# Layer 0's up projection with seven products for eight, its residual stream in DRAM during the MLP

## The chip, the cores and the metric

The kernel runs on one core of a Trainium2 chip (trn2). Its engines work side by side, each through its own instruction queue in order: TensorE (PE, matmuls), VectorE (DVE, elementwise work on tensors), ScalarE (ACT, functions and copies), GpSimd (POOL) and SyncE (SP), which issues most transfers. ACT and GpSimd can issue transfers too. The metric is the device time of one execution in microseconds (us); shorter is better.

## The reference

One inference step through two layers of a hybrid backbone, for 128 context tokens and 512 latent tokens, 640 in all, of 1024 channels. Each layer modulates its input with shift and scale rows made from a conditioning vector, projects it, runs three groups of heads (a two-way scan, a gated short convolution, a differential attention), projects back and adds:

```python
def trunk_layer(x, mod, p, ...):
    sh1, sc1, g1, sh2, sc2, g2 = jnp.split(mod, 6, axis=-1)
    u = x * (1.0 + sc1) + sh1
    m, k, v, s_f, s_b = mixer(u, p, ...)
    x = layer_norm(ALPHA * x + g1 * m, p['ln1_g'], p['ln1_b'])
    h = x * (1.0 + sc2) + sh2
    f = jnp.square(jax.nn.relu(h @ p['w_up'])) @ p['w_down']
    x = layer_norm(ALPHA * x + g2 * f, p['ln2_g'], p['ln2_b'])
    return x, k, v, s_f, s_b
```

`mod` is `silu(c) @ w_mod[l] + b_mod[l]`, with one `c` for the context tokens and one for the latent tokens; `w_mod[l]` is 1024 by 6144. The hidden width of the MLP is 4096. Everything is float32.

## The kernel before

Each float32 operand of a large product is split into a high part rounded to fp32r (by ACT) and a low part, the rest (a subtraction on DVE), and each product is three matmuls: high by high, high by low, low by high. `XH` and `XL` hold the split activations, channels on the partitions, tokens along the free axis. Weights come as 512 KB tiles through three `raw` buffers on SP's queue and are split into five buffers `hi` and `lo`.

`build` runs over the layers (L615). Its tools order each engine's instructions ahead of time, by a priority that follows the program's order; `tc.high_priority(offset=-LATE)` moves work behind. `fillers` are pieces of work that are threaded between others: `spread(n)` adds `n` to what is due and emits so many steps.

The end of a layer, which the change touches:

- Output projection `wo` (L1225 to L1232), in two blocks of 512 columns over five token tiles. `residual` multiplies the product with the gate row `grow` and adds the residual stream `res` (five tiles in SBUF, pool `rp`); `stats` makes mean and variance, with a power on GpSimd; `to_XT` transposes the normed tile into `XH`, `XL`. The LayerNorm's own scale and shift are applied to `res` later (`affine`, two DVE passes a tile).
- The MLP (L1441 on) goes through groups of hidden columns: up products, ReLU, square, split into `ah` and `al` (`squared`), then down products that are accumulated in `acc`.
  - Layer 0 (`fast` false): four groups of 1024, each of two plain up blocks (`up_block`: 192 matmuls, tokens as 384 + 256) and two down blocks (`tok_block`, one PSUM bank for each token tile, from the pair `mm`). The high part of the squares is a CAST on DVE (L1254).
  - Layer 1 (`fast` true): eight groups of 512. Group 0 is a plain up block, with the tokens as 320 + 320. Groups 1 to 7 are two calls of `fast_pair` each: the 2 x 2 block product of 256 hidden columns by 640 tokens, by halves of both and of the channels, with seven products (of 12 matmuls of 320 columns) for eight. It takes four sums of weights (`T1` to `T4`, made in each pair on DVE) and four sums of tokens. `token_sums` makes three of the latter once, in tiles `Sh`, `Sl` (the first two in `xn` buffers, six in `op`); `token_sums_in_place` writes the fourth over a quarter of `XH`, `XL`. `dn_fast` does the ten down products of a group, the first four halves in four PSUM banks (`mm` and `tp`).
- Layer 0 carries a filler through its MLP: `mod_steps_sum` makes seven modulation pieces (one of layer 0, six of layer 1) on DVE. Each of 112 tiles `ws` (256 KB, three buffers) is multiplied with two conditioning values and added into two accumulators `ma` (tag `xn`, two buffers): 28 first steps with one operand (L104), 196 with two (L109). PE then sums a piece over the partitions with a column of ones (`pmod`) and transposes it (`mod_tail`).
- At the last group, `acc` is multiplied by the second gate row and added to `res` (L1462 to L1465); the last down products come on top, with the LayerNorm. Layer 0 writes the result to `xspill` in DRAM, prepares layer 1's input (`put_u`) and starts its first product (`kv1`).

Of the kernel before, what the change touches and what calls it, by code (L numbers as in the profile page):

```python
# [35 lines left out]
FZ, FU, FD = 2, .7, 3  # L36
# [5 lines left out]
LATE, EARLY = 100, 50  # L42
# [3 lines left out]
ORDER, N_HALF = (4, 3, 0, 1, 2), 4  # L46
# [12 lines left out]
def build(ctx: ExitStack, tc: tile.TileContext, I, O):  # L59
# [159 lines left out]
    def mod_steps_sum(pieces, pool):  # L219
# [4 lines left out]
        def small(name):  # L224
            return pool.tile([P, 4, P], F32, tag="u", name=name, bufs=3).rearrange("p a b -> p (a b)")
# [11 lines left out]
        for l, pc in pieces:  # L237
            acc = [pool.tile([P, 1024], F32, tag="xn", name=f"ma{l}_{pc}_{s}", bufs=2) for s in range(2)]
# [220 lines left out]
    xspill = dp.tile([TOK, D], F32, name="xspill")  # L459

# [154 lines left out]
    for l in range(DEPTH):  # L615
# [553 lines left out]
        def stats(i, t):  # L1169
            mv = rp.tile([P, 4], F32, tag="mv", name=f"mv{l}_{i}_{t}", bufs=NT)  # L1170
# [5 lines left out]
        def stats_act(t):  # L1176

            mv = rp.tile([P, 4], F32, tag="mv", name=f"mv{l}_a{t}", bufs=NT)
# [37 lines left out]
        ubufs[0] = 5 if l + 1 == DEPTH else 3  # L1216
# [10 lines left out]
        if l + 1 < DEPTH:  # L1227
            next_end = ctx.enter_context(ExitStack())
            ep = next_end.enter_context(tc.tile_pool(name=f"kv{l + 1}", bufs=1, side=side_of(None), reuse_waits="tile"))
        op, op_end = open_pool("op")  # L1230
# [7 lines left out]
        fast = l + 1 == DEPTH  # L1238
        ng = 8 if fast else 4
        hg = 4 * D // ng  # L1240
        extra = {} if fast else {"more": op, "early": EARLY}
# [5 lines left out]
        def squared(r, hv, lv, src=None):  # L1247
# [12 lines left out]
        def up_block(g, b, ah, al):  # L1260
            blk = load_block(f"up{l}_{g}_{b}", w_up, 0, [(g * hg + b * 512, 512)], **extra)

            def ev_up(ct, half, ps):
                nm = f"relu{l}_{g}_{b}_{ct}_{half}"
                if fast:
                    o, m, r = half * H, H, room(nm)
                else:
                    o, m = (0, NA) if half == 0 else (NA, NB)
                    r = op.tile([P, NA], F32, tag="relu", name=nm, bufs=3)[:, :m]
# [3 lines left out]
            ch_block(f"up{l}_{g}_{b}", blk, ev_up, na=H if fast else NA)  # L1273
# [54 lines left out]
        def s_tile(name):  # L1328
# [83 lines left out]
        def dn_fast(g, stat, blks, evs):  # L1412

            items = [(t, c) for c in range(2) for t in ORDER]
            if g == ng - 1:
                items.sort(key=lambda x: ORDER.index(x[0]))
# [22 lines left out]

        ends = []  # L1440
        for g in range(ng):  # L1441
            ah, al = a_tiles(g, hg // P)
            if fast and g:
                for j in range(2):
                    fast_pair(g, j, ah, al)
                if g == ng // 2:
                    gate_rows(1)
            else:
                for b in range(hg // 512):
                    up_block(g, b, ah, al)  # L1450
                    if g == 0 and b == 0:
                        with tc.high_priority(offset=-LATE if fast else 0):
                            for t, mv in later:
                                affine(rows, t, mv)
                        if fast:
                            with tc.high_priority(offset=-LATE):
                                token_sums()
                    if g == ng // 2 and b == 0:
                        gate_rows(1)
                if fast:  # L1460
                    token_sums_in_place()
            if g == ng - 1:  # L1462
                for t in range(NT):
                    tt(acc[t], acc[t], grow[min(t, 1)], ALU.mult)
                    stt(res[t], res[t], ALPHA, acc[t], ALU.mult, ALU.add)  # L1465
                rows = norm_rows(1)
                if l + 1 < DEPTH:
                    fill_all()
                    make_aff(l + 1, 0, vt[:, 75:83], vt[:, 83:91])
            for cbi in range(2):  # L1470
                blk = load_block(f"dn{l}_{g}_{cbi}", w_down, g * hg, [(cbi * 512, 512)], nu=hg // 256, **extra)
# [5 lines left out]
                def ev_dn(t, ps, cbi=cbi, cs=cs, g=g):  # L1477
# [6 lines left out]
                    else:  # L1484
                        quiet = fast and t in ORDER[:-1]
                        residual(t, cbi, ps, None, not quiet)
                        if cbi == 1:
# [10 lines left out]
                            if l + 1 == DEPTH:  # L1498
                                end = t == ORDER[-1]
                                with tc.high_priority(offset=0 if end else -LATE):  # L1500
                                    finish(rows, 2 if end else 1)

                if fast:
                    ends.append((blk, ev_dn))
                else:
                    tok_block(f"dn{l}_{g}_{cbi}", blk, a_stat, ev_dn)
            if fast:
                dn_fast(g, a_stat, [e[0] for e in ends], [e[1] for e in ends])
                del ends[:]
# [67 lines left out]
```

## Time and profile before

| | |
|---|---|
| median of 3 runs | 1599.03 us (1595.26 to 1599.63) |
| the profiled execution | 1600.18 us, span of its records 1598.4 us |
| busy: PE, DVE, ACT, POOL | 1558.9, 1165.1, 768.6, 38.5 us |
| granted PE clock, mean | 0.995 of full speed |
| DMA | 201.47 MB, mean 126 GB/s |

PE rows give matmuls, PEld rows the loads of their stationary operand, which overlap them. Matmuls are pipelined and their ends are modelled, so the distance of their starts says more than their durations. L and a number is a line of the kernel; where a helper records all operations (L97 ACT copies and functions, L100 two-operand DVE passes, L109 scalar-tensor-tensor passes, L112 matmuls) the tile names say what it is. Layer 0's MLP runs from about 392 to 841 us, layer 1's from about 1167 to the end.

### The profile page before, as it was taken

To read this page: it belongs to the slowest core of one execution; us is meant where nothing else is said; L and a number is where in the kernel's file an instruction comes from. 1 tells how busy PE (TensorE), PEld (TensorE's weight loads), DVE (VectorE), ACT (ScalarE), POOL (GpSimd) and SP (SyncE) were. 2 spreads that over 40 slices of the span, in tenths; PEclk is the share of its full clock that TensorE was granted. 3 is DMA by queue.
4 is the path that set the end of the run, shared out by engine and by line. 5 is a ranking of instruction groups with operands and counts; after the bars stand their busy time and mean duration, and the time that the engine had idled before them with its cause. 6 is when DMAs were issued, how large, how long until landed. Compare 5 with 4: busy or idle time off the path is not lost.

```text
span 1598.4 us, 23756 instructions
## 1 busy us (share of the span) xinstructions
PE 1558.9 (98%) x9088; PEld 1373.1 (86%) x9088; DVE 1165.1 (73%) x2122; ACT 768.6 (48%) x1610; POOL 38.5 (2%) x68
## 2 busy tenths in 40 slices
PE   6999999999999999999999999999999999999997
PEld 3799957978989979979978999898798899988995
DVE  2589868778858478499376788898797566556687
ACT  3368735427422413314245587654486355434543
POOL 0000100000000000000000000000000000000001
PEclk9999999999999999999999999999999999999998
DMA  9641177342555355364226410524222233122311
GB/s 325 181 167 54 36 252 260 126 154 75 164 194 187 105 170 159 126 198 140 71 73 183 169 41 14 185 100 150 81 85 88 67 105 98 61 67 92 106 66 66
DMA packets 124833, 201.47 MB, mean 126 GB/s; under 512 B 10924, under 2 KB 57776, under 8 KB 124720
## 3 DMA queue, kind: packets, MB, share of 16 engines
q1 hardware_dynamic: 116592, 179.46, 35.0%
q10 hardware_dynamic: 8128, 20.50, 3.6%
q8 instruction: 71, 1.16, 0.3%
q14 instruction: 42, 0.34, 0.1%
HBM read 186.71 MB, written 13.22 MB: 125 GB/s over the span
## 4 chain that ended last, share of the span: by engine, by line
PE 86%; DVE 6%; DMA 3%; ACT 3%; issue 1%; POOL 1%; SPq 0%; DVEq 0%; ACTq 0%; POOLq 0%
PE dn_t L112 26%; PE up_c L112 15%; PE wo_t L112 4%; PE kv_t L112 4%; PE xb_c L112 4%; PE sa_c L112 3%; PE xa_c L112 3%; PE z_t L112 2%; PE pt L112 2%; PE px L1380 2%; PE px L1381 2%; PE px L1382 2%; PE dq_t L112 2%; PE pmod L112 2%; PE sb_c L112 2%; DVE res L109 1%
## 5 line engine op out<-in xcount | busy, mean ns | idle before, releaser
L112 PE MATMUL dn_t<-hdn,ah 128*128 128x512 f32 x640 | 251.2, 393 | 0.0
L112 PE MATMUL dn_t<-hdn,al 128*128 128x512 f32 x640 | 250.1, 391 | 0.0
L112 PE MATMUL dn_t<-ldn,ah 128*128 128x512 f32 x640 | 249.9, 390 | 0.0
L112 PE MATMUL up_c<-XH,hup 128*128 128x384 f32 (+2 forms) x576 | 178.3, 310 | 0.0
L112 PE MATMUL up_c<-XH,lup 128*128 128x384 f32 (+2 forms) x576 | 178.1, 309 | 0.1
L112 PE MATMUL up_c<-XL,hup 128*128 128x384 f32 (+2 forms) x576 | 178.1, 309 | 0.0
L109 DVE SCALAR_TENSOR_TENSOR ma<-ws,cstat,ma 128x512 f32<-128x512 f32 x196 | 138.1, 745 | 15.8 <-DMA ws<-in_w_mod_dram 15.1
L112 PEld LDWEIGHTS dn_t<-hdn,ah 128*128 128x128 f32 x640 | 120.2, 188 | 29.9 <-issue 2.5
L112 PEld LDWEIGHTS dn_t<-ldn,ah 128*128 128x128 f32 x640 | 120.2, 188 | 25.9
L112 PEld LDWEIGHTS dn_t<-hdn,al 128*128 128x128 f32 x640 | 120.2, 188 | 24.7
L112 PEld LDWEIGHTS up_c<-XH,lup 128*128 128x128 f32 x576 | 108.9, 189 | 0.8 <-DVE lup L100 0.7
L112 PEld LDWEIGHTS up_c<-XH,hup 128*128 128x128 f32 x576 | 108.1, 188 | 1.0 <-ACT relu L97 0.8
L112 PEld LDWEIGHTS up_c<-XL,hup 128*128 128x128 f32 x576 | 108.1, 188 | 0.5 <-DVE XL L100 0.2
L97 ACT ACTIVATE hdn<-rdn 128x1024 fp32r<-128x1024 f32 x64 | 66.9, 1053 | 79.7 <-PE dn_t L112 52.4
L100 DVE TENSOR_TENSOR ldn<-rdn,hdn 128x1024 fp32r<-128x1024 f32 x64 | 77.4, 1222 | 37.8 <-ACT hdn L97 37.7
L100 DVE TENSOR_TENSOR acc<-acc,dn_t 128x512 f32<-128x512 f32 x80 | 54.6, 683 | 56.5 <-PE dn_t L112 56.5
L97 ACT ACTIVATE relu<-up_c 128x384 f32<-128x384 f32 (+2 forms) x72 | 31.3, 434 | 112.1 <-PE up_c L112 105.0
L112 PE MATMUL wo_t<-hwo,XH 128*128 128x512 f32 x160 | 63.1, 394 | 1.5 <-ACT XH L97 1.5
L112 PE MATMUL wo_t<-hwo,XL 128*128 128x512 f32 x160 | 63.7, 398 | 0.0
L112 PE MATMUL wo_t<-lwo,XH 128*128 128x512 f32 x160 | 63.7, 398 | 0.0
L97 ACT ACTIVATE pe<-sc,zs 128x640 f32<-128x640 f32 (+1 forms) x80 | 56.8, 712 | 10.9 <-DVE pe L109 6.9
L844 DVE TENSOR_REDUCE zs<-sc 128x1 f32<-128x640 f32 x64 | 52.3, 820 | 12.5 <-PE sc L112 12.1
(413 smaller groups left out, 3913.2 us busy)
## 6 DMA issues: line engine op xcount, KB each, us to landing
rup<-in_w_up_dram SPq DMA_DIRECT2D x64, 512.0 KB
rdn<-in_w_down_dram SPq DMA_DIRECT2D x64, 512.0 KB
ws<-in_w_mod_dram SPq DMA_DIRECT2D x112, 256.0 KB
wm<-in_w_mod_dram SPq DMA_DIRECT2D x24, 512.0 KB
Ab<-adram SPq DMA_DIRECT2D x10, 1024.0 KB
rwo<-in_w_out_dram SPq DMA_DIRECT2D x16, 512.0 KB
wb<-in_w_mod_dram SPq DMA_DIRECT2D x12, 512.0 KB
kd<-hlks SPq DMA_DIRECT2D x40, 128.0 KB
```

Source lines behind the costliest of these rows:

```text
L97: S.activation(out=out, in_=in_, func=func, **kw)
L100: V.tensor_tensor(out=out, in0=a, in1=b, op=op)
L109: V.scalar_tensor_tensor(out=out, in0=a, scalar=s, in1=b, op0=op0, op1=op1, **kw)
L112: T.matmul(out, lhsT=l, rhs=r, start=start, stop=stop)
L844: V.tensor_reduce(out=nmax, in_=sv, axis=AX.XY, op=ALU.max, negate=True)
L1380: T.matmul(ps, lhsT=wh, rhs=xh, start=k == 0 and not more, stop=False, skip_group_check=more)
L1381: T.matmul(ps, lhsT=wh, rhs=xl, start=False, stop=False, skip_group_check=more)
L1382: T.matmul(ps, lhsT=wl, rhs=xh, start=False, stop=k == 3, skip_group_check=more)
```

## The change

Layer 0's MLP takes the form that layer 1 has: eight groups of 512, a plain up block in group 0, `fast_pair` in groups 1 to 7, `dn_fast` (now `dn_block`) for the down products. In both layers:

- after `affine` the five `res` tiles are written to DRAM (`mid`, on GpSimd's queue) and the pool `rp` is closed; a pool `sp` with six tiles `S0` to `S5` for the token sums takes its place;
- `before_last`, called between the two pairs of the last group, empties the fillers, loads the second gate rows, multiplies `acc` with them and adds ALPHA times the residual stream, which comes back from DRAM through the buffers `u` in halves of 512 columns (GpSimd's queue); `acc` then is `res`;
- the second LayerNorm's rows go into `S0` and `S1` (they went into `acc`);
- the gate rows share the buffers `ma` with the modulation sums, in `op`, which is opened ahead of the output projection (pool `gr` is gone); `ws` has a tag of its own.

The fillers are threaded otherwise (`FU` at each of four outputs of a pair, `FD` at each down product), the ring `u` has five buffers in both layers, layer 0's last group takes its token tiles in the order 0 to 4, and `EARLY` and the extra weight unit in `op` are gone. The diff, cut:

```diff
-FZ, FU, FD = 2, .7, 3
+FZ, FU, FD = 2, .8, 1.4
-ORDER, N_HALF = (4, 3, 0, 1, 2), 4
+ORDERS, N_HALF = ((0, 1, 2, 3, 4), (4, 3, 0, 1, 2)), 4
...
-            return pool.tile([P, 4, P], F32, tag="u", name=name, bufs=3).rearrange("p a b -> p (a b)")
+            return pool.tile([P, 512], F32, tag="ws", name=name, bufs=3)
...
-            acc = [pool.tile([P, 1024], F32, tag="xn", name=f"ma{l}_{pc}_{s}", bufs=2) for s in range(2)]
+            acc = [pool.tile([P, 1024], F32, tag="ma", name=f"ma{l}_{pc}_{s}", bufs=2) for s in range(2)]
...
+    mid = [dp.tile([TOK, D], F32, name=f"mid{l}") for l in range(DEPTH)]
...
-        gp, gp_end = open_pool("gr", "right")
+        op, op_end = open_pool("op")
...
-                r = gp.tile([P, D], F32, tag=f"grow{s}", name=f"grow{l}_{i}_{s}")
-                nc.scalar.dma_start(out=r, in_=gdram[l][i, s:s + 1, :].to_broadcast([P, D]))
+                r = op.tile([P, D], F32, tag="ma", name=f"grow{l}_{i}_{s}", bufs=2)
+                (nc.scalar, G)[i].dma_start(out=r, in_=gdram[l][i, s:s + 1, :].to_broadcast([P, D]))
...
-                r = acc[j]
+                r = acc[j] if i == 0 else sp.tile([P, D], F32, tag=f"S{j}", name=f"row{l}_{j}")
...
-        ubufs[0] = 5 if l + 1 == DEPTH else 3
+        ubufs[0] = 5
...
-        fast = l + 1 == DEPTH
-        ng = 8 if fast else 4
+        end = l + 1 == DEPTH
+        order = ORDERS[end]
+        ng = 8
...
-            if fast:
-                act(hv, r)
-            else:
-                V.tensor_copy(hv, r)
+            act(hv, r)
...
-                x = op.tile([P, 3 * H], F32R, name=name)
+                x = sp.tile([P, D], F32R, tag=f"S{len(made) - 3}", name=name)
...
             def out(r, ct, half, src=None):
+                spread(FU)
...
+        def before_last():
+            nonlocal rows
+            if l + 1 < DEPTH:
+                fill_all()
+            gate_rows(1)
+            for t in order:
+                a = acc[t]
+                tt(a, a, grow[min(t, 1)], ALU.mult)
+                for i in range(2):
+                    x, cs = flat(f"x{l}_{t}_{i}"), slice(i * 512, i * 512 + 512)
+                    G.dma_start(out=x, in_=mid[l][t * P:(t + 1) * P, cs])
+                    stt(a[:, cs], x, ALPHA, a[:, cs], ALU.mult, ALU.add)
+            res[:] = acc
+            rows = norm_rows(1)
+            if l + 1 < DEPTH:
+                make_aff(l + 1, 0, vt[:, 75:83], vt[:, 83:91])
...
-            if fast and g:
+            if g:
                 for j in range(2):
                     fast_pair(g, j, ah, al)
-                if g == ng // 2:
-                    gate_rows(1)
+                    if g == ng - 1 and j == 0:
+                        before_last()
...
-                        with tc.high_priority(offset=-LATE if fast else 0):
+                        with tc.high_priority(offset=-LATE):
                             for t, mv in later:
                                 affine(rows, t, mv)
+                                G.dma_start(out=mid[l][t * P:(t + 1) * P, :], in_=res[t])
+                        rp_end.close()
+                        sp, sp_end = open_pool("sp", "right")
+                        with tc.high_priority(offset=-LATE):
+                            token_sums()
...
-            if g == ng - 1:
-                for t in range(NT):
-                    tt(acc[t], acc[t], grow[min(t, 1)], ALU.mult)
-                    stt(res[t], res[t], ALPHA, acc[t], ALU.mult, ALU.add)
```

## Rows read from the trace of the kernel before

**Rows 1.** The page, part 1: busy time, share of the span and instructions of each engine.

```profile
PE 1558.9 (98%) x9088; PEld 1373.1 (86%) x9088; DVE 1165.1 (73%) x2122; ACT 768.6 (48%) x1610; POOL 38.5 (2%) x68
```

**Rows 2.** The chain of waits in order of time: start, length, what.

```profile
302.63 8.56 PE sb_c L112 x59
...
437.28 16.32 PE dn_t L112 x72
...
495.24 56.53 PE up_c L112 x384
...
841.31 10.99 PE kv_t L112 x48
...
1087.33 9.36 PE sb_c L112 x63
...
1194.82 27.48 PE dn_t L112 x120
1246.94 27.49 PE dn_t L112 x120
```

**Rows 3.** Busy time by stretch: length, PE, PEld, DVE, ACT, POOL, clock, DMA.

```profile
437.28:495.24 57.96, 57.96 (x267) 45.91 (x266) 36.28 (x56) 15.75 (x23) 0.00 (x0) 1.00 0.55 178
392.41:782.42 390.01, 389.57 (x2278) 351.77 (x2278) 279.07 (x456) 123.05 (x206) 0.00 (x0) 1.00 0.47 151
782.42:841.31 58.89, 57.80 (x266) 47.31 (x265) 40.76 (x62) 23.37 (x40) 1.62 (x3) 1.00 0.28 88
1167.54:1559.78 392.24, 392.24 (x2203) 357.14 (x2203) 263.04 (x430) 201.91 (x405) 2.05 (x1) 1.00 0.26 84
...
1507.54:1559.78 52.24, 52.24 (x289) 47.17 (x289) 41.56 (x58) 23.81 (x49) 0.00 (x0) 1.00 0.24 81
```

**Rows 4.** Grouped DVE instructions of layer 0's MLP, 395 to 841 us.

```profile
L109 DVE SCALAR_TENSOR_TENSOR ma<-ws,cstat,ma 128x512 f32<-128x512 f32 x196 | 138.1, 745 | 15.8 <-DMA ws<-in_w_mod_dram 15.1
...
L104 DVE TENSOR_SCALAR ma<-ws,cstat 128x512 f32<-128x512 f32 x28 | 11.9, 481 | 14.9 <-PE pmod L112 14.9
```

**Rows 5.** DVE in order of time in two dense runs: start, length, operation.

```profile
691.69 0.68 DVE L100 TENSOR_TENSOR acc<-acc,dn_t 128x512 f32<-128x512 f32 x1
692.29 1.41 DVE L109 SCALAR_TENSOR_TENSOR ma<-ws,cstat,ma 128x512 f32<-128x512 f32 x2
693.61 1.22 DVE L100 TENSOR_TENSOR ldn<-rdn,hdn 128x1024 fp32r<-128x1024 f32 x1
694.75 1.21 DVE L100 TENSOR_TENSOR lup<-rup,hup 128x1024 fp32r<-128x1024 f32 x1
...
1197.48 0.48 DVE L100 TENSOR_TENSOR Sl<-xa,Sh 128x320 fp32r<-128x320 f32 x1
1197.89 0.48 DVE L100 TENSOR_TENSOR xc<-xa,xc 128x320 f32<-128x320 f32 x1
```

**Rows 6.** Busy time by stretch, columns as in rows 3, of three dense runs.

```profile
1174.58:1217.44 42.86, 42.86 (x239) 38.45 (x238) 40.59 (x84) 30.51 (x63) 0.00 (x0) 1.00 0.18 58
686.06:725.43 39.37, 39.35 (x179) 31.48 (x179) 36.61 (x53) 7.62 (x8) 0.00 (x0) 1.00 0.63 197
...
664.14:724.94 60.80, 60.36 (x283) 47.94 (x283) 53.77 (x81) 12.55 (x16) 0.00 (x0) 1.00 0.61 191
```

**Rows 7.** Who waited for whom: us in total, times, longest.

```profile
DVE ma L109 <- DMA ws<-in_w_mod_dram: 15.1, 18, 2.0
DVE ma L104 <- PE pmod L112: 14.9, 4, 11.2
```

**Rows 8.** DVE in order of time, layer 1's first group.

```profile
1175.98 2.60 DVE L109 SCALAR_TENSOR_TENSOR res<-res,mv,acc 128x1024 f32<-128x1024 f32 x2 [0.51 <-ACT xn L97]
...
1189.21 0.48 DVE L100 TENSOR_TENSOR Sl<-xa,Sh 128x320 fp32r<-128x320 f32 x1
...
1215.97 1.47 DVE L100 TENSOR_TENSOR lo_T<-t,hi_T 128x512 fp32r<-128x512 f32 x2
```

**Rows 9.** The chain of waits, a weight tile of 512 KB.

```profile
350.45 4.29 DMA rup<-in_w_up_dram
```

More of the change, by code (lines that the diff above doesn't have):

```diff
@@ L1136, in build @@
         p1_end.close()
-        gp, gp_end = open_pool("gr", "right")
+        if l + 1 < DEPTH:
+            next_end = ctx.enter_context(ExitStack())
+            ep = next_end.enter_context(tc.tile_pool(name=f"kv{l + 1}", bufs=1, side=side_of(None), reuse_waits="tile"))
+        op, op_end = open_pool("op")
         grow = []
@@ L1169, in stats @@
         def stats(i, t):
[L1170 removed]
+            mv = op.tile([P, 4], F32, tag="mv", name=f"mv{l}_{i}_{t}", bufs=NT)
             V.bn_aggr(out=mv[:, 0:2], in_=st6[:, t].rearrange("p a b -> p (a b)"))
@@ L1176, in stats_act @@
         def stats_act(t):
-            mv = rp.tile([P, 4], F32, tag="mv", name=f"mv{l}_a{t}", bufs=NT)
+            mv = op.tile([P, 4], F32, tag="mv", name=f"mv{l}_a{t}", bufs=NT)
             x = op.tile([P, D], F32, tag="xn", name=f"dev{l}_{t}", bufs=2)
@@ L1260, in up_block @@
         def up_block(g, b, ah, al):
-            blk = load_block(f"up{l}_{g}_{b}", w_up, 0, [(g * hg + b * 512, 512)], **extra)
+            blk = load_block(f"up{l}_{g}_{b}", w_up, 0, [(g * hg + b * 512, 512)])
             def ev_up(ct, half, ps):
                 nm = f"relu{l}_{g}_{b}_{ct}_{half}"
[L1265 to L1269, printed above, removed]
+                o, m, r = half * H, H, room(nm)
                 squared(r, ah[4 * b + ct][:, o:o + m], al[4 * b + ct][:, o:o + m], ps)
                 spread(FU)
-            ch_block(f"up{l}_{g}_{b}", blk, ev_up, na=H if fast else NA)
+            ch_block(f"up{l}_{g}_{b}", blk, ev_up, na=H)
         quarter = {}
@@ L1410, in fast_pair, with dn_block @@
             out(room("c21" + nm), 0, 1, px)
-        def dn_fast(g, stat, blks, evs):
-            items = [(t, c) for c in range(2) for t in ORDER]
+        def dn_block(g, stat, blks, evs):
+            items = [(t, c) for c in range(2) for t in order]
             if g == ng - 1:
-                items.sort(key=lambda x: ORDER.index(x[0]))
+                items.sort(key=lambda x: order.index(x[0]))
             def part(i, ps, k0, k1):
@@ L1451, in build @@
                     if g == 0 and b == 0:
-                        with tc.high_priority(offset=-LATE if fast else 0):
+                        with tc.high_priority(offset=-LATE):
                             for t, mv in later:
                                 affine(rows, t, mv)
[L1455 to L1461, printed above, removed]
-            if g == ng - 1:
-                for t in range(NT):
-                    tt(acc[t], acc[t], grow[min(t, 1)], ALU.mult)
-                    stt(res[t], res[t], ALPHA, acc[t], ALU.mult, ALU.add)
[L1466 to L1469, printed above, removed]
+                                G.dma_start(out=mid[l][t * P:(t + 1) * P, :], in_=res[t])
[3 more added lines that the diff above has]
+                            token_sums()
+                token_sums_in_place()
             for cbi in range(2):
-                blk = load_block(f"dn{l}_{g}_{cbi}", w_down, g * hg, [(cbi * 512, 512)], nu=hg // 256, **extra)
+                blk = load_block(f"dn{l}_{g}_{cbi}", w_down, g * hg, [(cbi * 512, 512)], nu=hg // 256)
                 cs = slice(cbi * 512, (cbi + 1) * 512)
@@ L1484, in ev_dn @@
                     else:
-                        quiet = fast and t in ORDER[:-1]
+                        quiet = end and t in order[:-1]
                         residual(t, cbi, ps, None, not quiet)
@@ L1498, in ev_dn @@
                             if l + 1 == DEPTH:
[L1499 to L1509, printed above, removed]
+                                final = t == order[-1]
+                                with tc.high_priority(offset=0 if final else -LATE):
+                                    finish(rows, 2 if final else 1)
+                ends.append((blk, ev_dn))
+            dn_block(g, a_stat, [e[0] for e in ends], [e[1] for e in ends])
+            del ends[:]
         if l + 1 < DEPTH:
```

8 lines of the change are left out of this document (2 added, 6 removed).

## The prediction

> **What bounds the kernel now.** I read the page first: TensorE (PE) is busy 98% of the span, VectorE (DVE) 73% [rows 1]. An average over two layers says little about one stage, so I went on to the chain of waits. There the MLP of either layer is one unbroken run of matmuls: 384 up products in 56.53 us in layer 0, and in layer 1 down blocks of 120 products in 27.48 us that begin every 52.12 us [rows 2]. PE sets the end in both MLPs, and a product taken away is worth its time if nothing else becomes late. What could become late I read from the table of stretches: in layer 0's MLP DVE is busy 279.07 us of 390.01 up to the last down block, in layer 1's 263.04 of 392.24 [rows 3]. The grouped instructions say why layer 0 is so full although its MLP is the plain one: it also carries the weighted sums that make the modulation rows, 196 two-operand steps and 28 one-operand steps, 150.0 us together [rows 4]. Layer 1 has none. The question is whether layer 1's form of the MLP and these sums fit on DVE together.
>
> **The PE term.** One plain block of 512 hidden columns costs 56.53/2 = 28.27 us [rows 2]. The form with seven products costs what is left of layer 1's period: 52.12 - 27.48 = 24.64 us. Group 0 stays plain, so 7 groups x (28.27 - 24.64) = **25.4 us less**. The down products stay as many (8 groups of 120 for 4 of 240). The way into the MLP should not move: from the end of the last short-convolution product to the first down product layer 0 takes 437.28 - 311.19 = 126.1 us with two plain blocks inside, layer 1 takes 1194.82 - 1096.69 = 98.1 us with one [rows 2]; without that one block's 28.3 us the former is 97.8 us. So dropping `EARLY` and the extra unit in `op` is costed at nothing; what hides it is the PE work of the output projection, which is equally long in both.
>
> **The DVE term.** In a dense run what counts is the distance from start to start, since ends overlap: 0.40 us for 320 columns, 0.60 for 512, 1.14 for 1024, 0.66 for a modulation step of 512 [rows 5]; the one-operand step of a piece's first tile counts 0.40 (481 ns less the same overlap of 80) [rows 4], an `affine` pass 1.3 (2.60 for two) [rows 8]. I list what DVE must do in the changed layer 0 from the start of group 0's up block to the end of group 7's, by layer 1's counts:
> - 14 pairs, each 11 passes of 512 (four differences, seven low parts) and 7 of 320 (three sums, four low parts): 14 x 9.4 = 131.6
> - 56 passes of 320 for the token sums: 22.4
> - 32 splits of down weights x 1.14: 36.5
> - 60 accumulations x 0.60 (20 before): 36.0
> - group 0's low parts, the late `affine` passes and what is left of the projection: 13.0
> - gates and residual in `before_last`, 5 x 1.14 + 10 x 0.66: 12.3
> - modulation, 196 x 0.66 + 28 x 0.40 and small ones: 142.0
>
> Together 394 us. PE needs in the same stretch layer 1's 392.24 us [rows 3] and seven modulation pieces: layer 0's second stretch takes 57.96 us, with 2 x 27.48 = 54.96 of down products, some 0.7 of up and two pieces, so 1.15 us a piece [rows 2, 3], 8 us in all: 400.3 us. DVE would have to work **98% of the time** where it works 72% now. The casts of the squares go from DVE to ACT, and the list has none of them. ACT, with 23.81 of 52.24 us in a group of layer 1 [rows 3], has room, and costs nothing.
>
> How dense can DVE be? Two runs show it with all work ready: 40.59 of 42.86 us in layer 1's token sums and 36.61 of 39.37 in layer 0's modulation, so 94.7% and 93.0% [rows 6]. The gaps have two causes that stay: two accumulators `ma` for each piece, so that the next one waits for PE's column sum (14.9 us, 4 times), and three buffers `ws` (15.1 us, 18 times) [rows 7]. At these densities 394 us become 416 and 424, and PE would stand still for 16 to 23 us. The other end is nothing, since 394 is less than 400.3: a DVE that is late finds its inputs waiting, and a gap closes that in those runs only existed because nothing was due. I take **14 us**, nearer to the dense run that has the new form. Behind DVE the stall shows first at group 1, since the token sums and the first 20 modulation steps (6 in the up block, 14 in the down block) come ahead of its weights, where layer 1's run already ends only 5 us before the pairs begin at 1222.30 [rows 2, 8]; and at the end, where `gate_rows(1)` needs both `ma` and thus the last piece.
>
> **The last down block of layer 0.** It shrinks from 55 us to 27.5 and must take the same residuals. DVE is busy 40.76 us of the 58.89 at this place now [rows 3]; less half of the down splits (4 x 1.14) it has some 36 us of work for 27.5 of PE. PE runs on into `kv1` (10.99 us [rows 2]), which covers some of it. Bounds 0 and 8.5 us, the whole of the difference; taken: **4 us**.
>
> **The residual stream through DRAM.** Ten writes of 512 KB, twenty reads of 256 KB and four of the gate rows are issued by GpSimd, whose queue issues no transfer now and carries the power step of every LayerNorm. The writes gate the buffers `S`, which lie where `res` was. Landing bounds it: 512 KB of weights took 4.29 us [rows 9]. In layer 1 the last `affine` ends at 1178.6 and the first sums that would go into `S` come at 1189 [rows 8], so a write of 4.3 us is hidden with some 6 us to spare; late writes would hold the token sums, and these group 1. In `before_last` the x tiles come in among the five buffers `u` that the pair behind them also needs. Layer 1 does the same gates there now at no cost (52.24 us for the group, DVE 41.56 [rows 3]). Bounds 0 (all hidden) to 4.3 us a layer (one landing in the open); for both layers together **2 us**. `ma` for the gate rows of the first residual opens no new wait: its space is free once the scan is done, which comes before the projection.
>
> The Trainium skill speaks against this part. "SBUF — State Buffer", SBUF: two separate sides, says that a transfer issued by GpSimd has its descriptors written by that engine, and that a DVE copy, cast or one-operand step in SBUF locks it out meanwhile. The only ops of that kind left in layer 0's MLP would be the 28 one-operand steps of 481 ns, and no run of before has a GpSimd transfer that could show it; by the rule a write waits at most one such step, so the sum would be 1 to 2 us more.
>
> **Sum.** - 25.4 + 14 + 4 + 2 = - 5.4 us. The profiled execution took 1600.18 us, its span and 1.8 around it; it lies 1.15 us above the median of the three runs, 1599.03. Against itself 1594.8, against the median 1593.6: I forecast **1595 us**. About 0.3% (4.8 us) is what a measurement of this kernel can tell from no change, so the forecast stands at that edge.
>
> **Rivals.**
> 1. *DVE keeps up.* For it: in layer 1 no group loses PE time although its first stretch is 94.7% dense [rows 6], and there are five buffers for split weights, half a group of lead. Against it: 98% of the time is more than any run shows. Stall 0 to 5, little at the end: 1577 to 1586, say 1581.
> 2. *DVE becomes the bound and costs more than PE gives* (the other side). One mechanism: DVE's order is fixed, and a waiting step at its head (`ma` for PE, for `ws`) holds the weights of the next pair behind it. The longest stretch that is full, 664.14 to 724.94, has DVE at 53.77 of 60.80 us, 88.4% [rows 6]: 394 us would be 446, a stall of 45 and 1626 us. It decides from a density of 93.9% downward, where the stall passes 25.4 - 6 = 19.4 us, and from 92.8% by more than 0.3%. Against it: in that stretch DVE had no need to be denser, since PE waited for it almost nowhere. Typical 1612.
> 3. *The x reads come late.* They wait for buffers `u` and for GpSimd; each reads 256 KB behind the others. If ten of them land one after the other at half of 4.3 us each, they take 21 us from the moment at which the first buffer is free, of which the 24.64 us of the last pairs and the first half products hide all but what begins late. One landing of 4.3 us in the open at each layer's end, and as much for the token that follows: 8 us more than forecast, 1603.
> 4. *The seven column sums of the modulation stop PE,* because the down block now rotates through both pairs of PSUM banks and leaves none for them. One product group of 2.75 us (27.48/10) for each: 19 us, 1614. For it: `dn_block` takes four banks; against it: they are held for one matmul and one copy only.
>
> By a rule of "DMA: Bandwidth & Descriptors" in the Trainium skill, Anatomy of one DMA, a GpSimd transfer takes about 2 us and its bytes at 436 GB/s, an estimate of 2.6 us for 256 KB; ten in a row would be 26 us, and rival 3 is where that would show.
>
> **Chances.** Forecast 0.42 (stall 6 to 20 us: 1587 to 1601), rival 1 0.20, rival 2 0.23, rival 3 0.10, rival 4 0.05. The forecast's own range spans the edge: of its 0.42 half is faster by over 0.3%, 0.15 within, 0.06 slower. Rival 1 is all faster; rival 2 is slower but for 0.02; rival 3 is mostly within (0.06 to 0.04); rival 4 slower but for 0.01. That gives faster 0.41, same 0.24, slower 0.35. The range 1579 to 1614 leaves out the quicker third of rival 1 and the worse half of rival 2, a little under 2 in 10.
>
> **What will show it.** PE: pairs at 24.6 us where nothing is late, and 168 more lines of px, py and pz per group. DVE in layer 0's MLP over 90% in every group, where now 72%; if its busy share is high and PE's falls under 100% there, the DVE term is right, and the idle time of PE ahead of hi and lo tiles (or of `ma`) is its size. The last `ma` should stand in group 6 or 7, not, as now, one down block ahead of the end. Wrong would be: PE waiting on `S` tiles or on x (rivals 3), pairs that are slower by themselves, or DVE at a share under 90% with PE stalled. Layer 1 should be as long as before within 2 us.

## The result, and the profile after

| | before | after |
|---|---|---|
| median | 1599.3 us (4 runs, 1595.26 to 1599.63) | 1622.85 us (4 runs, 1620.29 to 1625.25) |
| span of the profiled execution | 1598.4 | 1618.3 |

The change makes the kernel slower: ratio 1.0148, 95% interval 1.0125 to 1.0172. The forecast was 1595 us, the range 1579 to 1614: wrong in sign, and outside the range. The profiled execution of the changed kernel, from which the numbers below come, is the shortest of its four: 1620.29 us at a mean granted clock of 0.992; the longest, 1625.25 us, shows 0.989.

The page of the kernel after, part 1, answers to [rows 1]: DVE is busy 78% of the span for 73, PE 96% for 98.

```profile
PE 1560.5 (96%) x8920; PEld 1353.8 (84%) x8920; DVE 1267.3 (78%) x2332; ACT 836.6 (52%) x1802; POOL 58.7 (4%) x102
```

Where the 19.9 us of the spans lie, by PE's starts. A is the stretch from layer 0's last short-convolution product (sb) to `kv1`, with the projection and the whole MLP; B from there to layer 1's last sb product; C layer 1's last group, from its first pair to the last down product. In brackets is what the granted clock took: the sum over windows of 10 us of length times (1 - clock).

| | A | B | C | the rest |
|---|---|---|---|---|
| before | 528.1 (0) | 257.4 (3.4) | 52.0 | 760.9 |
| after | 535.7 (1.7) | 265.9 (6.8) | 55.3 | 761.4 |
| forecast of the difference | -6.4 | 0 | +1 | 0 |

(A's -6.4 is -25.4 + 14 + 4 + 1: the 2 us of the residual stream are taken as 1 in A and 1 in C.)

Inside A, the way from sb to the first down product went from 124.1 to 97.3 us, 26.8 less where one block's 28.3 were forecast. (The prediction's 126.1 and 97.8 count from 311.19, where the chain of waits leaves sb; its last product starts at 313.06.) From the first down product to `kv1` it took 438.5 for 404.0. The table of stretches of the kernel after shows that DVE is far fuller than the 72% of [rows 3], if not at the 98% of the forecast: 90 to 95% in a group up to 760 us (shown are group 0 with the start of group 1, group 2, group 6, and the stretch as a whole):

```profile
410.00:474.20 64.20, 57.80 (x291) 47.69 (x290) 57.95 (x105) 32.70 (x68) 0.00 (x0) 0.97 0.40 127
474.20:531.20 57.00, 57.00 (x302) 48.02 (x301) 52.26 (x87) 23.83 (x48) 0.00 (x0) 1.00 0.49 155
705.40:760.10 54.70, 54.69 (x302) 47.77 (x301) 52.21 (x91) 24.68 (x51) 0.00 (x0) 1.00 0.50 159
...
410.00:848.63 438.63, 428.88 (x2250) 361.42 (x2249) 398.13 (x675) 198.34 (x399) 8.13 (x15) 1.00 0.46 147
```

But PE is hardly idle in groups 2 to 6, and they are long all the same (54.7 to 60.1 us; layer 1's 52.07). PE in order of time in group 2 shows one reason: the eight `pmod` matmuls of a modulation piece, 1.06 us in one lot before, now come, in five of the seven pieces, as lots of 2, 4 and 2, of about 1.0 us each, between products that need 0.147 from start to start; the one behind a lot needs 0.26.

```profile
504.27 1.04 PE L112 MATMUL pmod<-ma,one 128*32 128x512 f32 x2
505.24 0.41 PE L1373 MATMUL px<-Sh,hi_T 128*128 128x320 f32 x1
505.50 0.31 PE L1374 MATMUL px<-Sl,hi_T 128*128 128x320 f32 x1
505.64 0.31 PE L1375 MATMUL px<-Sh,lo_T 128*128 128x320 f32 x1
...
507.20 1.05 PE L112 MATMUL pmod<-ma,one 128*32 128x512 f32 x4
...
508.97 1.04 PE L112 MATMUL pmod<-ma,one 128*32 128x512 f32 x2
```

Summed from start to start, the 438.5 us are: down products 960 x 233.3 ns = 224.0 (before 960 x 227.2 = 218.1), pairs 1176 x 146.7 = 172.5 (before three groups of up products, 169.6), `pmod` 16.9 (before 7.0), transposes 5.2 (5.1), and 19.9 (4.2) of waits and slow first matmuls behind a wait or a lot. Waits of more than 0.2 us are 11.7 of the 19.9: 7.6 at group 1, 2.5 at the last pair, 1.6 between. The waits of PE from 410 to 475 us (us in total, times, longest):

```profile
PE px L1375 <- DVE lo_b L100: 2.7, 1, 2.7
PE pmod L112 <- DVE ma L109: 1.7, 2, 1.5
PE px L1373 <- ACT s L97: 1.2, 1, 1.2
```

B shows in SP's queue. In order of time from 838 us, first before, then after, and third the wait of SP there (us in total, times, longest): the loads of `rdq` stand ahead of the cache loads and of the writes of layer 1's keys (`kcd`, `kd`), in both. In the kernel after, the last of them wait 14.0 us for a `raw` buffer that the first split `ldq` on DVE frees. The keys come 13.9 us later, where `kv1` is 7.3 later, and PE waits 2.4 us at 885 in front of their transposes.

```profile
838.90 7.49 SPq L348 DMA_DIRECT2D rdq<-in_w_in_dram  x6
846.48 0.42 SPq L748 DMA_DIRECT2D k<-in_cache_k_dram  x1
...
861.17 1.95 SPq L690 DMA_DIRECT2D kcd<-hlkc  x4
```

```profile
850.64 22.06 SPq L348 DMA_DIRECT2D rdq<-in_w_in_dram  x8
872.81 0.69 SPq L749 DMA_DIRECT2D k<-in_cache_k_dram  x1
...
875.10 2.11 SPq L691 DMA_DIRECT2D kcd<-hlkc  x4
```

```profile
SPq L348 <- DVE ldq L100: 14.0, 1, 14.0
```

C is the x reads (10 in each layer, a median of 3.4 us from issue to landing). GpSimd's queue in layer 1's last group, after: four reads are issued at once, then it waits 13.89 us for a buffer `u`, since DVE, in its order, takes the first x only behind all five gates (1553.32). The last pair's sums of weights need `u` too; PE waits 1.9 us for them (second fence, the waits of PE).

```profile
1537.81 1.19 POOL L1445 DMA_DIRECT2D x<-mid  x2 [341.99 <-DVE lo_T L100]
1539.37 1.15 POOL L1445 DMA_DIRECT2D x<-mid  x2 [0.37 <-DVE lo_T L100]
1554.41 1.17 POOL L1445 DMA_DIRECT2D x<-mid  x2 [13.89 <-DVE acc L109]
```

```profile
PE pz L1373 <- ACT hi_T L97: 1.9, 1, 1.9
```

### The profile page after: what moved, and what is told of

It reads as the page before. It is cut to its first block, busy times and chain, and to the rows that moved or that the text cites. A ratio compares the mean times of both kernels' runs of the same rounds, so it can differ in the third digit from the quotient of the medians.

```text
span 1618.3 us, 23902 instructions
## 1 busy us (share of the span) xinstructions
PE 1560.5 (96%) x8920; PEld 1353.8 (84%) x8920; DVE 1267.3 (78%) x2332; ACT 836.6 (52%) x1802; POOL 58.7 (4%) x102
## 3 DMA queue, kind: packets, MB, share of 16 engines
q8 instruction: 70, 1.15, 0.3%
## 4 chain that ended last, share of the span: by engine, by line
PE 44%; DVE 3%; DMA 2%; issue 2%; ACT 1%; SPq 0%; POOL 0%; DVEq 0%; ACTq 0%; POOLq 0%
PE dn_t L112 15%; PE wo_t L112 2%; PE px L1373 2%; PE px L1375 2%; PE px L1374 2%; PE xb_c L112 2%; PE sa_c L112 2%; PE z_t L112 1%; PE kv_t L112 1%; PE xa_c L112 1%; PE pt L112 1%; PE pz L1375 1%; PE up_c L112 1%; PE pz L1374 1%; PE pz L1373 1%
## 5 line engine op out<-in xcount | busy, mean ns | idle before, releaser
L100 DVE TENSOR_TENSOR acc<-acc,dn_t 128x512 f32<-128x512 f32 x140 | 95.4, 683 | 63.9 <-PE dn_t L112 63.0
L97 ACT ACTIVATE hi_T<-t 128x512 fp32r<-128x512 f32 x112 | 67.6, 626 | 122.5 <-DVE t L100 87.7
L100 DVE TENSOR_TENSOR lo_T<-t,hi_T 128x512 fp32r<-128x512 f32 x112 | 74.0, 685 | 17.3 <-ACT hi_T L97 17.2
L97 ACT ACTIVATE hi_b<-rup 128x512 fp32r<-128x512 f32 x56 | 33.6, 623 | 104.1 <-PE dn_t L112 94.2
L1373 PE MATMUL px<-XH,hi_T 128*128 128x320 f32 x224 | 70.0, 312 | 1.0 <-DVE p L100 0.8
L1374 PE MATMUL px<-XL,hi_T 128*128 128x320 f32 x224 | 69.1, 309 | 0.0
L1375 PE MATMUL px<-XH,lo_T 128*128 128x320 f32 x224 | 69.1, 308 | 0.0
L109 DVE SCALAR_TENSOR_TENSOR cv<-cb,vecs,cv 128x642 f32<-128x642 f32 x64 | 56.1, 879 | 2.0 <-ACT cv L97 1.6
```

What stands on the lines that cost most here:

```text
L97: S.activation(out=out, in_=in_, func=func, **kw)
L100: V.tensor_tensor(out=out, in0=a, in1=b, op=op)
L109: V.scalar_tensor_tensor(out=out, in0=a, scalar=s, in1=b, op0=op0, op1=op1, **kw)
L1373: T.matmul(ps, lhsT=wh, rhs=xh, start=k == 0 and not more, stop=False, skip_group_check=more)
L1374: T.matmul(ps, lhsT=wh, rhs=xl, start=False, stop=False, skip_group_check=more)
L1375: T.matmul(ps, lhsT=wl, rhs=xh, start=False, stop=k == 3, skip_group_check=more)
```

## The experiments

Each is an edit of the changed kernel. A, B and C are the stretches above, in brackets the part of the granted clock; ratios are to the kernel before. The stretches are of one profiled execution each, which is not the median one: e11's is the longest of its six (1596.91 us), e12's the shortest of its five (1588.03).

| run | median | ratio, 95% interval | A | B | C |
|---|---|---|---|---|---|
| the change | 1622.85 | 1.0148 (1.0125 to 1.0172) | 535.7 (1.7) | 265.9 (6.8) | 55.3 |
| e1_no_sums | 1611.74 (one run) | | 524.5 (6.8) | 266.0 (5.1) | 56.3 |
| e2_one_lot | 1615.37 | 1.0095 (1.008 to 1.011) | 528.1 (6.8) | 266.1 (5.1) | 56.2 |
| e3_sum_in_s | 1611.81 | 1.0073 (1.0057 to 1.009) | 536.9 (1.7) | 256.9 (0) | 56.0 |
| e4_x_ring | 1621.1 | 1.0131 (1.0116 to 1.0147) | 537.4 (3.4) | 266.8 (6.8) | 52.0 |
| e5_spill_normed | 1631.66 | 1.0207 (1.0188 to 1.0225) | 535.1 (1.7) | 263.0 (5.1) | 56.2 |
| e6_group0_free | 1614.12 | 1.0091 (1.0076 to 1.0106) | 526.9 (5.1) | 267.6 (8.5) | 56.2 |
| e7_three | 1617.58 | 1.0114 (1.0099 to 1.0129) | 529.1 (5.1) | 260.1 (1.7) | 52.0 |
| e8_pad | 1623.1 | 1.015 (1.0133 to 1.0167) | 534.5 (3.4) | 266.6 (5.1) | 56.5 |
| e9_dq_early | 1616.46 | 1.0099 (1.0083 to 1.0115) | 535.2 (0) | 262.7 (5.1) | 55.5 |
| e10_x_behind | 1618.13 | 1.0109 (1.0096 to 1.0122) | 535.5 (1.7) | 265.7 (5.1) | 52.0 |
| e11_all | 1592.19 | 0.9953 (0.9939 to 0.9966) | 519.5 (6.8) | 259.1 (0) | 52.0 |
| e12_all_fd18 | 1589.89 | 0.9951 (0.9936 to 0.9966) | 517.8 (0) | 255.4 (0) | 52.0 |
| e13_all_fd18_act | 1594.03 | 0.9966 (0.9954 to 0.9978) | 521.1 (0) | 254.7 (0) | 52.0 |

**e1_no_sums.** The 196 two-operand steps go.

```diff
-                            else:
-                                stt(a, w, cst_c[:, k, s:s + 1], a, ALU.mult, ALU.add)
```

> Leaves out the 196 two-operand modulation steps on DVE (so seven modulation pieces hold only their first row block); their loads, first steps, column sums and transposes stay. In the changed kernel the stretch from layer 0's first down product to the start of kv1 takes 438.7 us, DVE is busy 398 of it, and start to start the pairs lose 15.6 us to waits and refills. If a saturated DVE makes PE wait, DVE falls to about 262 us there and the waits go: 7 us at the start of group 1, 2 to 3 us at the last pair, 1 to 2 us between; the stretch shrinks by 9 to 15 us, and by as much as 23 if DVE also slows the down products (233.3 ns from start to start in layer 0, 229.0 in layer 1): then these fall to 229 or 227. If the column sums, not DVE, cost the time, the stretch shrinks by under 5 us and pmod still takes 2.4 us a piece. If the down products' 233.3 ns have another cause than DVE's load, they stay.

**e2_one_lot.** The four column sums of a piece stand behind the last one in PE's order (`column(g)` is the old matmul).

```diff
-            for g in range(4):
-                mm(ps[32 * g:32 * g + 32, :], one, ...)
+            lead = column(3)
+            with tc.issue_after(lead.ins):
+                for g in range(3):
+                    column(g)
```

> The four column sums of a modulation piece are issued one behind the other, after the one whose input is ready last; nothing else changes. If what they cost is that each lot takes PE about 1.0 us, whether one or four of them run, and refills the pipeline behind it, pmod falls from 16.9 us in layer 0's MLP to about 8 and the neighbours' loss from 7 to 3: 9 to 13 us less, 1610 to 1614 us. If the scheduler had split them because PE would otherwise wait for the last modulation step of DVE, the saving goes into a wait on ma: within 3 us of the changed kernel.

A fell by 11.2 us in e1 and by 7.6 in e2. In e1 the scheduler also put the column sums together (`pmod` 7.0 us, in e2 7.8), so e2 is the one to compare e1 with: both lose 6.8 us of A to the clock, and e1 is 3.6 us shorter there. That is less than what the steps cost in the MLP, since in e1 PE waits 5.5 us for `xn` in the projection, ahead of the MLP, where in e2 it waits 1.3; from group 1 to `kv1` e1 takes 392.6 us for 405.2, some 3.6 of it because it has done 11 more down products and a lot of column sums before. The stretches from group 2 to group 7, first of e1, then of e2 (289.0 us in the changed kernel):

```profile
507.00:779.60 272.60, 271.77 (x1503) 238.13 (x1502) 170.15 (x289) 124.23 (x247) 3.23 (x6) 1.00 0.50 156
```

```profile
503.20:781.60 278.40, 277.99 (x1527) 241.38 (x1526) 263.52 (x443) 123.94 (x250) 3.23 (x6) 1.00 0.52 161
```

In these five groups the split lots cost 10.6 us, and DVE at 94.7%, not 62%, costs 5.8, little over 1 us a group. The down products ran at 233 ns in both, so DVE's load does not set their pace.

**e3_sum_in_s.** Layer 0's last sums of tokens 1 to 4 go to S tiles.

```diff
+                if l + 1 < DEPTH and t:
+                    if cbi == 0:
+                        moved[t] = sp.tile([P, D], F32, tag=f"S{t + 1}", ...)
+                    tt(moved[t][:, cs], res[t][:, cs], ps, ALU.add)
```

> Layer 0's last sums (stream plus MLP) of tokens 1 to 4 go to the tiles S2 to S5 instead of into acc, so that the space of acc, which layer 1's attention tiles take over, is free without waiting for the late affine passes and the spill. From kv1's start to layer 1's dq it takes 39.4 us in the changed kernel, 30.3 before. If space is the cause, 6 to 9 us come back there. If DVE is (it works without a gap from 824 to 871 us, the ten affine passes among it, ahead of the split ldq that SP's queue waits 14.0 us for), nothing comes back: within 2 us.

B came back by 9.0 us, to 256.9: 6.8 of it from the clock, which no longer falls (below), and 2.2 from waits. The space of `acc` is a cause. Not all of the wait went: SP's queue waits 2.4 us for `ldq`, and then 7.2 us for the spill, now out of the S tiles.

**e4_x_ring.** `x` is taken from the ring of three buffers `ws`, idle by then, in both layers: `op.tile([P, 512], F32, tag="ws", ...)` for `flat(...)`.

> The x reads of both layers' last group go through the three buffers ws (idle there) instead of the five buffers u, which the last pair also needs for its sums of weights. If the wait for u is what holds up the last pair (2.0 and 2.1 us before pz, layer 1's last group 80.25 us for 76.97 before), both waits go and layer 1's last group comes back to 77 to 78: 4 to 7 us less in all. If DVE's order is (the ten stream passes ahead of the pair's low parts), the waits stay: within 2 us of the changed kernel.

C returned to 52.0 and PE waits for nothing there: in layer 1 the buffers are the cause. Layer 0's last group grew by 2 us (58.2 to 60.2 up to `kv1`): the stream's passes now come early and stand ahead of the pair's `p`, for which PE waits 2.9 us. These 2 us come from DVE's order (e10).

**e5_spill_normed.** Layer 0 spills `xn`, layer 1 applies scale and shift.

```diff
+            nc.scalar.dma_start(out=xspill[t * P:(t + 1) * P, :], in_=xn)
...
+                    for x in res:
+                        tt(x[:, cs], x[:, cs], r, o)
```

> Layer 0 spills the normed rows that ACT makes anyway; the LayerNorm's own scale and shift are applied in layer 1 after the reload (twenty DVE passes of 512 there for ten of 1024 at layer 0's end). So both the ten affine passes ahead of the split ldq and the wait for the space of acc go. From kv1's start to the first xa product it takes 52.1 us in the changed kernel, 46.4 before, 49.7 with the sums in S; on to the end of sb 213.8, 211.0 and 207.2. If DVE's ten passes are what holds ldq, and with it SP's queue (14.0 us), kv1 to xa comes to 46 to 47 and the granted clock no longer falls between 880 and 920 us: 9 to 11 us less in all, 1610 to 1613. If space alone was it, it equals the run with the sums in S: 49 to 50 to xa. If layer 1's added passes come late for the first residual, the projection of layer 1 loses what is won.

This is slower than the change: the twenty passes come late in layer 1. The waits of PE from 1080 to 1240 us, first of e5, then of the changed kernel:

```profile
PE pz L1131 <- DVE XL L100: 6.8, 4, 3.3
```

```profile
PE pz L1123 <- DVE XL L100: 0.4, 1, 0.4
```

From its last sb product to group 1 layer 1 lost 11.1 us (135.3 for 124.2), 5.1 of it by the clock, which takes nothing there in the changed kernel. B came back by 2.9 only, 1.7 of it the clock's: DVE now idles 5.2 us at 856, and SP still waits 10.9 us for `ldq`, which stands behind tokens 3 and 4 in DVE's order. So the passes as such are little of the cause.

**e6_group0_free.** No `spread` in group 0; `FD` 1.6 for 1.4.

> No modulation step is threaded through group 0 (FD 1.6 for 1.4 makes up for it in the later groups). In the changed kernel PE waits at the start of group 1 for low parts, for ma and for ACT: 2.85, 0.24, 0.38, 1.67, 0.69 and 1.37 us, 7.2 in all. If the token sums and the 20 modulation steps ahead of group 1's weights are the cause, 5 to 7 us go there. If DVE is saturated all the way through, the steps come later and PE loses as much in groups 2 to 7: within 3 us in all. If only the order counts, about 4 us are won.

From group 1 to group 2 it took 51.5 us for 66.0, with no wait of PE there (2.8 us of the difference are 12 down products that now come later); A fell by 8.8. The pieces now end in group 7, and the last group pays: 74.6 us up to `kv1` for 58.2, 5.1 of them by the clock. The waits of PE from 755 us:

```profile
PE pz L1372 <- ACT hi_T L97: 5.4, 1, 5.4
PE dn_t L112 <- ACT c L97: 1.5, 1, 1.5
```

**e7_three.** e2, e5 and the ring of e4 in layer 1 alone.

> Three edits together: the column sums in one lot (7.5 us less when alone), the normed rows spilled (9 to 11 expected), and x reads through the idle buffers ws in layer 1 alone (there 3.3 us less, in layer 0 2 us more). If the three places add up, 1599 to 1603 us, as long as the kernel before. If one theory of the three is only a shift of the same stall, 1607 to 1612.

A fell as in e2, C as in e4, and the loss of e5 came along. Added to the changed kernel, what the three gave alone (-7.5, -3.3 and +8.8 us) makes 1620.9 us; 1617.58 was measured, outside both of the expected ranges. So the places add up within 3.3 us, but one of them was a loss.

**e8_pad.**

```diff
+        if l == 0:
+            pad = op.tile([P, 8], F32, name="pad")
+            V.memset(pad, 0.0)
```

> A spare tile of 32 bytes at the head of layer 0's pool op; nothing else. The down products run at 233.3 ns from start to start in the changed layer 0, at 227.2 in layer 0 before and 229.0 in layer 1, and without the modulation sums on DVE they stay at 233. Of the four placements of ah and al, only the slow one begins at a multiple of 64 bytes; the others lie 32 bytes off. If the place in SBUF sets the pace, it falls to 227 to 229 with the spare tile: 960 products, 4 to 6 us less. If not, it stays 233 and the time stays within 2 us of the changed kernel.

The pace fell to 229.3 ns. PE in order of time, e8, then the changed kernel:

```profile
481.83 0.39 PE L112 MATMUL dn_t<-hdn,al 128*128 128x512 f32 x1
...
483.21 0.39 PE L112 MATMUL dn_t<-hdn,al 128*128 128x512 f32 x1
```

```profile
479.72 0.40 PE L112 MATMUL dn_t<-hdn,al 128*128 128x512 f32 x1
...
481.12 0.40 PE L112 MATMUL dn_t<-hdn,al 128*128 128x512 f32 x1
```

Six products take 1.38 us, or 1.40. That is 3.8 us over 960. The run's median did not fall; A did by 1.2, and by 2.9 without the clock's part. The pace itself is clear: it is 233.3 or 233.4 ns in every run without the spare tile, and 229.2 or 229.3 in all four with it (e8, e11 to e13).

**e9_dq_early.** `load_block(f"dq{l}", ..., early=400 * l)`.

> The splits of layer 1's dq weights get a higher priority; with it the first of them, which frees the raw buffer that SP's queue waits for, stands ahead of tokens 3 and 4 in DVE's order, as in the kernel before; nothing else. From kv1's start to xa 52.1 us in the changed kernel (46.4 before), and from there to the end of sb 213.8 (211.0). If the place of that one split is what holds SP's queue (14.0 us) and behind it the writes of kcd and kd, SP's wait goes, kv1 to xa comes to 46 to 48, and 5 to 9 us come back in all: 1612 to 1616. If the space of acc holds the loads behind it as well, SP waits as long for the next one: within 2 us of the changed kernel in this stretch.

SP's wait for `ldq` is gone, B fell by 3.2 (1.7 of it the clock's), and the next wait shows in the waits of SP from 840 to 880:

```profile
SPq L691 <- DMA xspill<-acc: 8.4, 4, 6.4
```

So it is both: the place of one split, and behind it the space of `acc`.

**e10_x_behind.** The ring of e4 and `tc.high_priority(offset=-LATE)` around `before_last`'s loop.

> The gates and the stream's passes of the last group stand about 100 instructions later in DVE's order, behind the sums of weights of the last pair, and the x reads go through the three idle buffers ws, in both layers. In layer 0 the ring alone gave nothing (last pair to kv1 60.2 us for 58.2), in layer 1 3.3 us. If DVE's order and the buffers u together hold up the last pair, layer 0's last stretch falls to 54 to 56 and layer 1's to 52: 5 to 8 us less than the changed kernel, 1613 to 1617. If the end of the modulation pieces (gate rows behind the last column sum) holds it, layer 0 keeps its 58 and only layer 1's 3.3 us come.

C is 52.0 and layer 0's last group 58.0, the figures of the second case. With the passes moved behind, e4's 2 us are gone. But the wait of PE that is left there, 1.5 us for `u` on ACT, does not name the modulation pieces, so what keeps the 58 is not shown.

**e11_all.** e2, e3, e6, e8, e9, e10 together.

> All the edits that helped alone, together: column sums in one lot, nothing threaded through group 0, the 32-byte shift of op, sums of layer 0 into S, dq's splits early, stream passes behind the last pair's sums. If the terms are separate places (7.5, 7, 4, 6, 5 and 5 us), they sum to 25 to 34 us less than the changed kernel: 1587 to 1597, below the kernel before. If DVE is the bound of layer 0's MLP after all, work that is moved only waits elsewhere, and it stays at 1600 to 1608.

This is faster than the kernel before. Groups 3 to 5 take 53.9 us each, which is layer 1's 52.07 and 1.8 for one piece's sums, transposes and what they slow behind them. The last group pays as in e6: 73.5 us from its start to `kv1`. There DVE waits at the head of its queue for x (in order of time):

```profile
793.78 0.69 DVE L109 SCALAR_TENSOR_TENSOR acc<-x,acc 128x512 f32<-128x512 f32 x1 [3.94 <-DMA x<-mid]
796.48 0.69 DVE L109 SCALAR_TENSOR_TENSOR acc<-x,acc 128x512 f32<-128x512 f32 x1 [2.00 <-DMA x<-mid]
```

**e12_all_fd18.** As e11 with `FD` 1.8.

> As the kernel with all edits, with FD 1.8 for 1.6, so that the modulation pieces end half a group earlier, in group 6 and not in the last group's first pair (last ma at 768.5 us, last pair's group from 762.5 us). There the gates, which need both ma, and the x reads behind them came late: 73.5 us from the start of group 7 to kv1 for 58.2 in the changed kernel, with PE waits of 6.8 and 2.5 us. If the late end of the pieces is the cause, these 15 us shrink to 0 to 5; groups 2 to 6 have DVE busy 52.1 of 54 us and get 2.7 us more each: if DVE then is the bound they become 55 to 56 us, otherwise they stay at 54. In sum 1580 to 1588 us; 1592 if the one takes what the other gives.

**e13_all_fd18_act.** In e12, `act(a, w, scale=cst_c[:, k, s:s + 1])` for the first steps on DVE.

> As the run before it, with the 28 one-operand first steps of the modulation sums (480 ns each, 11 to 13 us) on ACT, which is busy 24 of 54 us in these groups. If DVE's work bounds layer 0's groups now, they shrink by up to 2 us each, 5 to 11 us in all. If PE is the bound again, the time stays within 3 us. If ACT, whose order is fixed too, waits for ws at its head, the pairs wait for ACT and it is slower by 3 to 10 us.

In e12 the last group falls to 57.0 us, as expected, and groups 2 to 6, with the denser pieces, grow from 271.6 to 283.3 in all; the clock's 6.8 us of A are gone. Of the 11.7 us, 1.0 are one more piece's column sums; PE waits 8.4 us there for work of DVE and ACT, where it waited 1.2 in e11. That is the case of the expectation in which DVE bounds. The medians of e11 and e12 lie 2.3 us apart, and their intervals cover each other. In e13, which was to test it, DVE has 8.3 us less to do from group 1 to `kv1`, and that stretch is no shorter. The stretches from group 1 to `kv1`, e12, then e13, and third what ACT waits for in e13's:

```profile
436.50:830.70 394.20, 384.52 (x2129) 335.78 (x2128) 367.69 (x620) 182.47 (x364) 8.13 (x15) 1.00 0.50 157
```

```profile
438.50:835.60 397.10, 384.94 (x2128) 335.75 (x2127) 359.36 (x596) 195.10 (x388) 8.13 (x15) 1.00 0.49 155
```

```profile
ACT ma L97 <- PE pmod L253: 17.6, 3, 8.6
```

The moved steps now stand at the head of ACT's queue and wait there for the column sums, the third case of the expectation, and the median is 4.1 us higher. So e13 does not settle whether DVE, at 93%, bounds e12's stretch, of which PE is busy 97.5%.

## Why the prediction was wrong

- **The PE term, -25.4 us: right.** Without the other losses a group of layer 0 takes what layer 1's does, plus its piece (e11: 53.9). The pairs took the 172.5 us costed (7 x 24.64); the way into the MLP gave 26.8 for 28.3, so 23.9 were saved.
- **The column sums, "1.15 us a piece", "8 us in all", as before: this step failed.** They cost 16.9 us for 7.0, and the matmuls behind each lot as well; e2 gave back 7.6 us of A, 12.7 without the clock's part. Rival 4 named the place, but by PSUM banks; what happened is that the halves of a piece finish at different times, and the order made ahead of time puts each sum where its half is ready.
- **The stall of PE by DVE, 14 us: near in size and in its places, wrong in its working.** It came to 11.7 us of waits and the slow matmuls behind them. The step "PE would stand still for 16 to 23 us" at densities of 93 to 95% did not hold: at 94.7% (e2) DVE's load costs 5.8 us in five groups. Nor did "The gaps have two causes that stay": DVE's 15.1 and 14.9 us of [rows 7] fell to 3.6 and 3.3 (changed kernel, 395 to 849 us, below), as the prediction's other end said. That the size came out near is thus partly luck. What it said of group 1 and of the end held: token sums and 20 steps ahead of group 1's weights cost 7.6 us of waits, which e6 removed, and the last pair 2.5.

```profile
DVE ma L109 <- DMA ws<-in_w_mod_dram: 3.6, 7, 1.0
DVE ma L104 <- PE pmod L112: 3.3, 3, 1.3
```

- **The down products, costed as before: failed, unforeseen.** 227.2 to 233.3 ns, 5.9 us. e8 shows that the place of layer 0's pool in SBUF accounts for 4.0 ns of the 6.1.
- **The last down block, 4 us of 0 to 8.5: mis-sized, and not by its mechanism.** Most of it showed up behind `kv1`: B grew by 8.5, 3.4 of it by the clock. "PE runs on into `kv1` ..., which covers some of it" overlooked what stands behind `kv1`: SP's queue, held by one split's place on DVE (e9: 3.2 us with the clock's part), and the space of `acc`, which is now the stream and is taken over by layer 1 (e3: 9.0 us with the clock's part). The affine passes as such were little of it (e5). With it "Layer 1 should be as long as before within 2 us" failed: B and C grew by 11.8 us.
- **The residual stream, 2 us (0 to 4.3 a layer): inside its bounds.** 3.3 us in layer 1. Rival 3's landings (a median of 3.4 us, where the prediction estimated 2.6) were not the cause; the buffers `u` were (e4). The lock that "SBUF — State Buffer" of the Trainium skill names (SBUF: two separate sides) is not tested by them: GpSimd's issues in layer 1's last group took 0.55 us each, DVE at work or not, but DVE's passes beside them had two operands, and the lock was forecast for copies, casts and one-operand steps.
- **The sum.** In A it came out 14.0 us over the forecast: 9.9 (column sums), 5.9 (pace), 1.5 (products saved, 23.9 for 25.4), less 3.3 (waits and slow first matmuls 15.7 us over before, for 19 forecast). Behind A 8.5 and 2.3 more. That is 24.8 of the 25.3 us between -5.4 and the 19.9 of the spans. The medians lie 23.6 us apart, 3.7 more than the spans, because the profiled execution of the changed kernel lies 2.6 us below its median and that of the kernel before 0.9 above.

Reads of x with more than three buffers of their own were not tried, nor an `FD` between e11's and e12's.

## What to carry to other kernels

An engine at 95% cost 1 us a group here. What costs more is where the order around it is fixed: so look, for each engine and queue, at what stands at its head when the work is compressed, and at whose buffers it holds. When a small product's inputs finish at different times, tie its matmuls to the last one. When a tile gets a second life (`acc` as the stream), check who takes over its space, and when.

## What the runs showed of the hardware

- **Column groups side by side.** Eight `pmod` matmuls on four column groups of 32 take 1.06 us when issued together, four of them 1.05 us and two of them alone 1.04 us: a lot of two costs what a lot of eight does. That matmuls on column strips of 32 run side by side is what "TensorEngine Tiling (Array Packing)" of the Trainium skill says (Tiling Modes); the other half, that a strip alone is no cheaper, is the trace's.
- **The place in SBUF changes a matmul's pace.** With layer 0's pool moved by 32 bytes, the down products (512 columns, stationary `ah` and `al`) went from 233.3 to 229.3 ns. In the built programs the slow place is the only one of those compared in which `ah` and `al` begin at a multiple of 64 bytes. One shift was tried, and it moved every tile of the pool; the rule behind it is open, and so are the 2 ns to the 227.2 of before.
- **The clock.** What the granted clock's falls take from A and from B is nothing, 1.7 us or a multiple of it in every profiled execution, and nothing in the two together only in e12 and e13. Two stretches of B, changed kernel and then e3: in the first PE is idle 2.55 us and the mean clock is 0.83, between the two levels of 1.2 and 2.4 GHz, and 0.69 some 30 us later; with 1.30 us of idle time it stays at 2.4 GHz. Idle time alone does not decide it: in e7 (third) PE is idle 3.66 us and the clock stays at 2.4 GHz. What lets it fall at 910 us, where PE is busy, the runs do not show.

```profile
880.00:890.00 10.00, 7.45 (x45) 6.81 (x44) 4.81 (x12) 3.83 (x9) 0.00 (x0) 0.83 0.94 272
...
910.00:920.00 10.00, 10.00 (x49) 9.51 (x49) 6.18 (x18) 5.59 (x17) 0.00 (x0) 0.69 0.37 109
```

```profile
880.00:890.00 10.00, 8.70 (x57) 7.72 (x56) 5.45 (x13) 4.01 (x9) 0.00 (x0) 1.00 0.91 271
...
910.00:920.00 10.00, 10.00 (x71) 9.02 (x71) 7.67 (x25) 6.98 (x22) 0.00 (x0) 1.00 0.19 57
```

```profile
1012.80:1022.80 10.00, 6.34 (x29) 4.79 (x28) 6.75 (x11) 4.63 (x12) 0.00 (x0) 1.00 0.70 230
```
